# Summing the weights of paired columns by accumulating transfers from GpSimd instead of on VectorE, with two more pairs

## The chip, the core and the metric

The kernel runs on one core of one Trainium2 chip. Its time is the time on the device in microseconds (us), and less is better. In the text PE is TensorE, DVE is VectorE, ACT is ScalarE, POOL is GpSimd and SP is the SyncE queue that issues most transfers. L12 is line 12 of the kernel before.

## What is computed

A decoder trunk of two layers on 528 tokens (512 and 16 learned ones in front) of width 1024. Each layer has a mixer (one projection into two groups of four heads, an output projection) and then a gated MLP, which is where the change lies:

```
def _conv_ffn(h, ffn_up, ffn_conv_w, ffn_conv_b, ffn_down):
    length = h.shape[1]
    u = h @ ffn_up
    up = jnp.pad(u, ((0, 0), (CONV_W - 1, 0), (0, 0)))
    conv = ffn_conv_b + sum(up[:, i:i + length] * ffn_conv_w[i] for i in range(CONV_W))
    a, g = jnp.split(conv, 2, axis=-1)
    return (jax.nn.gelu(a, approximate=True) * g) @ ffn_down
...
    for i in range(DEPTH):
        m = _mixer(_rmsnorm(h, pre_mix_norm[i]), ...)
        h = h + _rmsnorm(m, post_mix_norm[i])
        f = _conv_ffn(_rmsnorm(h, pre_ffn_norm[i]), ffn_up[i], ffn_conv_w[i], ffn_conv_b[i], ffn_down[i])
        h = h + _rmsnorm(f, post_ffn_norm[i])
```

`ffn_up` is 1024 x 5632 per layer in float32: 22 columns of 128 for `a` and 22 for `g`. Column i of `a` and column i of `g` belong together, because their results are multiplied.

## The kernel before

**Products.** Activations lie with the model's width on the 128 partitions and the tokens along the free dimension. Every float32 product is made of float16 parts: a weight is split into a high and a low half, and so is the activation, and three matmuls (high by high, high by low, low by high) stand for one. ACT makes the high half of a weight (an ACTIVATE with a scale), DVE the low one (a SCALAR_TENSOR_TENSOR).

**Blocks.** `plan` lists every weight block of the program in the order of its use. A plain block is 1024 rows by 128 columns (`Block`): one load of 512 KB on SP (L104) into a float32 buffer ("stage cell", `st`), one conversion on ACT (L123) and one on DVE (L131) into a float16 buffer (`unit`). There are ten `unit` buffers (`UNITS`), taken in turn in the order of the blocks, so a block is converted when PE has finished with the block ten places earlier. There are eight stage cells for layer 0 and five for layer 1 (`STAGES`), also taken in turn; a load goes out as soon as its cell has been converted, so loads run further ahead than conversions. `block` asks for up to ten blocks beyond the one in use (`AHEAD`). Loads on SP keep the program's order. ACT and DVE take most of their work in an order that the compiler's list scheduler fixes ahead of the run; each engine then goes through its own list strictly in turn, and an instruction that waits holds up all behind it on that engine.

**A plain column of the up projection** is two blocks, `a` and `g` (`one` in `ffn_up`), each multiplied by the tokens in two parts: 0 to 232 (from 14 on in layer 1) and 232 to 528. ACT copies each product out of PSUM (L1353). After both blocks, `finish` runs the convolution (ACT L1337, DVE L1342), the Gelu (ACT L1393), the product of both (DVE L1404) and, in layer 0, its split into float16 parts (ACT L463, DVE L464).

**A pair** does the same two columns by Strassen's method in Winograd's form, with seven products in place of eight. The weights of column i are seen as a 2 x 2 block matrix: rows 0 to 511 and 512 to 1023 by column `a` and column `g`, so w11, w12 (upper half of `a` and `g`), w21, w22 (lower half). The tokens are halved too (264 each). Seven products of four row blocks of 128, with three matmuls each (12 matmuls over 264 tokens), need w11, w22, w21 and these sums: w11 + w12, w12 + w22, w11 + w12 + w22, and the sum of all four. `paired` runs the products, ACT copies three of them out of PSUM (L1304) and one result (L1326), DVE makes three sums of products (L1308). The sums of activations are made once per layer by `input_sums`. Columns 0 to 4 are always plain; `PAIRED` says which of the others are pairs.

**The weights of a pair** come as four pieces (`PairPiece`), each a unit of its own, taken in the order of steps 0 to 3: w11 with w22; w11 + w12 with w12 + w22; w11 + w12 + w22 with w21; the sum of all four. The products use them in the order 0, 1, 2, 0, 1, 2, 3. At step 0 four loads of 256 KB (L209) fill two stage cells, [w11, w22] and [w12, w21]. At steps 1 to 3 DVE adds in place with four TENSOR_TENSORs (L215), and ACT (L230) and DVE (L231) convert: one conversion of 1024 elements per partition at step 0, two of 512 at steps 1 and 2, one at step 3. Both cells are held until step 3 has been converted.

**Order around it.** PE's order is the compiler's as well: a pair's last product (12 matmuls) often runs inside the next column. PSUM has three banks for these products; the first product's bank is used again by the third. A dependency written by hand (`"sums first"` in `paired`) keeps a piece ten places ahead from being converted before the third product has been copied. POOL takes part in the norms (L459, L492, L514) before and after the up projections, and in L1468, two transfers of 256 KB at the end of the second one.

Of the kernel before, what the change touches and what calls it, by code (L numbers as in the profile page):

```python
# [9 lines left out]
F32 = mybir.dt.float32  # L10
U8 = mybir.dt.uint8
AF = mybir.ActivationFunctionType  # L12
ALU = mybir.AluOpType

P = 128
# [30 lines left out]
SLOTS = 41  # L46
AHEAD = 10
# [21 lines left out]
PAIRED = {0: (9, 11, 13, 14, 15, 17, 19, 20, 21), 1: (8, 10)}  # L69
HK2 = KD // 2  # L70
# [117 lines left out]
class PairPiece:  # L188
# [10 lines left out]

    def fetch(self):  # L200
        if self.unit is not None:
            return
        kern, nc = self.kern, self.kern.nc
        if self.step == 0:
            self.st = []
            for half in (((0, 0), (1, 1)), ((0, 1), (1, 0))):
                st = cell(kern.stage, [P, 2, HK2, P], F32, *kern.stage_of(self.layer))
                for i, (a, b) in enumerate(half):
                    load = nc.sync.dma_start(st[:, i], self.src[512 * a : 512 * (a + 1), self.cols[b] : self.cols[b] + P].rearrange("(k p) c -> p k c", p=P))  # L209
                    kern.tc.keep_in_program_order(load)  # L210
                self.st += [st[:, 0], st[:, 1]]
                if len(self.st) == 2:
                    self.both = st
        w = self.first.st
        add = lambda to, x: nc.vector.tensor_tensor(out=w[to], in0=w[to], in1=w[x], op=ALU.add)  # L215
        if self.step == 0:
            parts = [(slice(0, 2), self.both)]
        elif self.step == 1:
            add(0, 2)
            add(2, 1)  # L220
            parts = [(0, w[0]), (1, w[2])]
        elif self.step == 2:
            add(0, 1)
            parts = [(0, w[0]), (1, w[3])]
        else:
            add(0, 3)
            parts = [(0, w[0])]
        u = self.unit = cell(kern.wpool, [P, 2, 2, HK2, P], F16, "unit", "unit", UNITS)
        for i, st in parts:
            self.hi = nc.scalar.activation(u[:, 0, i], st, AF.Copy, scale=SW)  # L230
            nc.vector.scalar_tensor_tensor(out=u[:, 1, i], in0=st, scalar=SW, in1=u[:, 0, i], op0=ALU.mult, op1=ALU.subtract)  # L231


class Kern:
# [495 lines left out]
    def plan(self):  # L730
        a = self.a
# [7 lines left out]
        for l in range(DEPTH):  # L739
# [4 lines left out]
            for i in range(KF):  # L744
                if i in PAIRED[l]:
                    first = None
                    for q in range(4):
                        self.key[l, "pair", i, q] = len(self.blocks)
                        self.blocks.append(PairPiece(self, l, a["ffn_up"][l], (P * i, DFF + P * i), q, first))
                        first = first or self.blocks[-1]  # L750
                    continue
# [889 lines left out]
```

## Time and profile before

| | |
|---|---|
| median of 3 runs | 1195.14 us (1195.05 to 1195.2) |
| profiled execution | 1195.35 us, span 1193.5 us |
| granted TensorE clock | 1.000 |
| PE, DVE, ACT, POOL busy | 99%, 74%, 57%, 15% |
| HBM read, written | 120.24 MB, 2.10 MB |
| loads of `ffn_up`, plain | 66 of 512 KB, median 4.8 us to landing |
| loads of `ffn_up`, pairs | 44 of 256 KB, median 3.4 us to landing |

The span is the time from the first to the last instruction of the profiled execution; a little lies around it. The page gives busy shares, busy time in 40 slices of the span (about 30 us each), DMA queues, the chain of work that ended last, the costliest groups of instructions, and DMA issues with their time to landing. Other views answer for a stretch of time alone. Matmuls are pipelined: one shows 0.27 us although the next starts after about 0.11 us, so a pair is timed by the distance between its matmuls' starts. Pairs are the groups of line L1296. They lie from 362 to 495 us in layer 0 and from 940 to 973 us in layer 1.

### The profile page before, as it was taken

To read this page: it belongs to the slowest core of one execution; us is meant where nothing else is said; L and a number is where in the kernel's file an instruction comes from. 1 tells how busy PE (TensorE), PEld (TensorE's weight loads), DVE (VectorE), ACT (ScalarE), POOL (GpSimd) and SP (SyncE) were. 2 spreads that over 40 slices of the span, in tenths; PEclk is the share of its full clock that TensorE was granted. 3 is DMA by queue.
4 is the path that set the end of the run, shared out by engine and by line. 5 is a ranking of instruction groups with operands and counts; after the bars stand their busy time and mean duration, and the time that the engine had idled before them with its cause. 6 is when DMAs were issued, how large, how long until landed. Compare 5 with 4: busy or idle time off the path is not lost.

```text
span 1193.5 us, 26242 instructions
## 1 busy us (share of the span) xinstructions
PE 1183.8 (99%) x10910; PEld 998.4 (84%) x10910; DVE 879.8 (74%) x1539; ACT 682.5 (57%) x1351; POOL 184.1 (15%) x213
## 2 busy tenths in 40 slices
PE   8999999999999999999999999999999999999998
PEld 8888889989888888988888888899888888886445
DVE  6687855368998999833565968553799998797687
ACT  6685444564876676633346854445657676664452
POOL 2132311263000000000331414012620000000000
PEclk9999999999999999999999999999999999999999
DMA  8933131122613242642235132211422453206371
GB/s 224 276 108 96 54 90 54 37 65 78 177 36 89 77 119 74 184 112 77 80 99 142 55 89 72 72 54 37 124 71 72 125 164 110 99 1 225 117 250 71
DMA packets 207066, 124.02 MB, mean 104 GB/s; under 512 B 6928, under 2 KB 194500, under 8 KB 206948
## 3 DMA queue, kind: packets, MB, share of 16 engines
q1 hardware_dynamic: 206356, 121.37, 34.8%
q8 instruction: 85, 1.39, 0.5%
q0 software_dynamic: 160, 0.52, 0.1%
q10 hardware_dynamic: 432, 0.46, 0.1%
q14 instruction: 33, 0.27, 0.1%
HBM read 120.24 MB, written 2.10 MB: 103 GB/s over the span
## 4 chain that ended last, share of the span: by engine, by line
PE 87%; DVE 3%; issue 1%; ACT 1%; POOL 1%; POOLq 0%; DVEq 0%; ACTq 0%
PE pu L535 10%; PE pu L534 10%; PE pu L536 10%; PE pl L1480 8%; PE pp L1296 7%; PE pj L534 6%; PE pj L535 6%; PE pj L536 6%; PE pd L534 3%; PE pd L536 3%; PE pd L535 3%; PE po L534 2%; PE po L536 2%; PE po L535 2%; PE o L851 1%
## 5 line engine op out<-in xcount | busy, mean ns | idle before, releaser
L536 PE MATMUL pu<-every,unit 128*128 128x296 f16 (+2 forms) x1056 | 289.1, 274 | 0.0
L535 PE MATMUL pu<-every,unit 128*128 128x296 f16 (+2 forms) x1056 | 289.0, 274 | 0.0
L534 PE MATMUL pu<-every,unit 128*128 128x296 f16 (+2 forms) x1056 | 288.7, 274 | 0.0
L534 PEld LDWEIGHTS <-unit 128*128 128x128 f16 x2508 | 246.1, 98 | 35.4
L536 PEld LDWEIGHTS <-unit 128*128 128x128 f16 x2508 | 245.3, 98 | 36.2
L535 PEld LDWEIGHTS <-unit 128*128 128x128 f16 x2508 | 245.3, 98 | 35.5
L534 PE MATMUL pj<-every,unit 128*128 128x296 f16 (+2 forms) x888 | 244.3, 275 | 0.0
L535 PE MATMUL pj<-every,unit 128*128 128x296 f16 (+2 forms) x888 | 244.3, 275 | 0.0
L536 PE MATMUL pj<-every,unit 128*128 128x296 f16 (+2 forms) x888 | 244.2, 275 | 0.0
L131 DVE SCALAR_TENSOR_TENSOR unit<-st,unit 128x1024 f16<-128x1024 f32 (+2 forms) x161 | 196.7, 1229 | 43.5 <-ACT unit L123 43.3
L123 ACT ACTIVATE unit<-st 128x1024 f16<-128x1024 f32 x159 | 164.9, 1041 | 44.9 <-PE pd L536 20.4
L459 POOL TENSOR_TENSOR every<-every 128x5 f32<-128x5 f32 (+6 forms) x31 | 37.3, 1205 | 556.3 <-DVE every L458 463.2
L1296 PEld LDWEIGHTS <-unit 128*128 128x128 f16 x924 | 90.4, 98 | 14.0 <-issue 0.4
L492 DVE TENSOR_TENSOR acc<-acc,sq 128x296 f32<-128x296 f32 (+2 forms) x60 | 32.3, 541 | 75.0 <-ACT sq L490 69.5
L536 PE MATMUL pd<-av,unit 128*128 128x232 f16 (+1 forms) x308 | 84.7, 276 | 0.0
L535 PE MATMUL pd<-av,unit 128*128 128x232 f16 (+1 forms) x308 | 84.6, 276 | 0.0
L534 PE MATMUL pd<-av,unit 128*128 128x296 f16 (+1 forms) x308 | 84.4, 276 | 0.0
L1353 ACT ACTIVATE u<-pu 128x296 f32<-128x296 f32 (+2 forms) x132 | 49.8, 378 | 49.2 <-PE pu L536 48.0
L1480 PE MATMUL pl<-unit,fk 128*128 128x512 f16 x330 | 71.4, 379 | 0.0
L1342 DVE SCALAR_TENSOR_TENSOR cg<-u,every,cg 128x527 f32<-128x527 f32 (+1 forms) x88 | 66.3, 754 | 4.7 <-ACT cg L1337 4.3
L536 PE MATMUL po<-merged,unit 128*128 128x296 f16 (+2 forms) x256 | 69.7, 274 | 0.0
L535 PE MATMUL po<-merged,unit 128*128 128x296 f16 (+2 forms) x256 | 69.7, 274 | 0.0
(279 smaller groups left out, 1938.9 us busy)
## 6 DMA issues: line engine op xcount, KB each, us to landing
st<-in_ffn_up SPq DMA_DIRECT2D x66, 512.0 KB, 4.8
st<-in_w_in SPq DMA_DIRECT2D x56, 512.0 KB, 4.1
st<-in_ffn_down SPq DMA_DIRECT2D x46, 512.0 KB, 4.9
st<-in_ffn_up SPq DMA_DIRECT2D x44, 256.0 KB, 3.4
st<-in_w_out SPq DMA_DIRECT2D x16, 512.0 KB, 4.1
st<-in_ffn_down SPq DMA_DIRECT2D x8, 384.0 KB, 6.7
out<-yo SPq DMA_DIRECT2D x7, 256.0 KB, 2.0
w<-in_ffn_down SPq DMA_DIRECT2D x3, 512.0 KB, 5.1
```

What stands on the lines that cost most here:

```text
L123: self.hi = self.kern.nc.scalar.activation(self.unit[:, 0], self.st, AF.Copy, scale=SW)
L131: self.last = self.kern.nc.vector.scalar_tensor_tensor(out=out, in0=x, scalar=SW, in1=high, op0=ALU.mult, op1=ALU.subtract)
L459: nc.gpsimd.tensor_tensor(out=r[:w, :n], in0=t[:w, :n], in1=self.mhalf[:w, :n], op=ALU.pow)
L492: self.summed = eng.tensor_tensor(out=acc[:, :n], in0=acc[:, :n], in1=sq[:, :n], op=ALU.add)
L534: nc.tensor.matmul(ps[:, :n], w[:, 0, kk, :], x[:, 0, n0:n1], start=first, stop=False)
L535: nc.tensor.matmul(ps[:, :n], w[:, 0, kk, :], x[:, 1, n0:n1], start=False, stop=False)
L536: nc.tensor.matmul(ps[:, :n], w[:, 1, kk, :], x[:, 0, n0:n1], start=False, stop=last)
L851: nc.tensor.matmul(o[:, i, :], intra(i + 1), vn(i + 1), start=i == 0, stop=i == 0, skip_group_check=i > 0)
L1296: mm = lambda p, q, **kw: nc.tensor.matmul(ps, u[:, p, k, :], x[k][:, q], skip_group_check=more, **kw)
L1342: nc.vector.scalar_tensor_tensor(out=to, in0=u[:, max(lo, d) - d : L - d], scalar=self.cvec[:, ci(i) : ci(i) + 1], in1=to, op0=ALU.mult, o ...
L1353: nc.scalar.activation(u[:, n0:n1], ps[:, : n1 - n0], AF.Copy, scale=IXW)
L1480: mm = lambda x, w, **kw: nc.tensor.matmul(ps[:, cols], x, w[:, cols], skip_group_check=more, **kw)
```

## The change

Three things.

1. The sums are no longer made by DVE. `load` issues six loads of 256 KB on SP: w11 and w22, w12 and w21 as before, and w11 twice more into a third buffer [wa, wd]. That buffer is a cell of its own in layer 0 (`wx`, four of them, in the `keep` pool) and a third stage cell in layer 1. `sums` issues transfers from POOL that add to what lies in their destination (`accum_op`). At step 0: w12, once more from HBM, to wa; w22 to w12; w21 to wd; then the new w12 to wd. At step 1: the new w12 to w11. They keep the program's order on POOL. The pieces that are converted have the same values as before: wa is w11 + w12, the new w12 is w12 + w22, the new w11 is w11 + w12 + w22, wd is the sum of all four.
2. In `plan` each pair's first piece changes places with the block ahead of it (the `g` block of a plain column, or the last piece of the pair ahead), so it is loaded and converted one place earlier.
3. `PAIRED` in layer 0 goes from nine columns to ten, two pairs and then a plain column, with four pairs at the end; in layer 1 from two columns to three.

```diff
+WX = 4
...
-PAIRED = {0: (9, 11, 13, 14, 15, 17, 19, 20, 21), 1: (8, 10)}
+PAIRED = {0: (9, 10, 12, 13, 15, 16, 18, 19, 20, 21), 1: (8, 10, 12)}
...
+    def load(self):
+        kern, nc = self.kern, self.kern.nc
+        more = (kern.keep, "wx", "wx", WX) if self.layer == 0 else (kern.stage, *kern.stage_of(self.layer))
+        cells = [cell(pool, [P, 2, HK2, P], F32, *tag) for pool, *tag in [(kern.stage, *kern.stage_of(self.layer))] * 2 + [more]]
+        quarter = lambda a, b: self.src[512 * a : 512 * (a + 1), self.cols[b] : self.cols[b] + P].rearrange("(k p) c -> p k c", p=P)
+        order = ((0, 0, 0, 0), (0, 1, 1, 1), (1, 0, 0, 1), (2, 0, 0, 0), (1, 1, 1, 0), (2, 1, 0, 0))
+        for c, i, a, b in order:
+            load = nc.sync.dma_start(cells[c][:, i], quarter(a, b))
+            kern.tc.keep_in_program_order(load)
+        (w11, w22), (w12, w21), (wa, wd) = ((c[:, 0], c[:, 1]) for c in cells)
+        self.parts = [(slice(0, 2), cells[0])], [(0, wa), (1, w12)], [(0, w11), (1, w21)], [(0, wd)]
+        self.adds = [(wa, quarter(0, 1)), (w12, w22), (wd, w21), (wd, w12)], [(w11, w12)], [], []
+
+    def sums(self, step):
+        for to, x in self.adds[step]:
+            add = self.kern.nc.gpsimd.dma_start(out=to, in_=x, accum_op=ALU.add)
+            self.kern.tc.keep_in_program_order(add)
+
     def fetch(self):
...
-        w = self.first.st
-        add = lambda to, x: nc.vector.tensor_tensor(out=w[to], in0=w[to], in1=w[x], op=ALU.add)
-        if self.step == 0:
-            parts = [(slice(0, 2), self.both)]
-        elif self.step == 1:
-            add(0, 2)
-            add(2, 1)
-            parts = [(0, w[0]), (1, w[2])]
-        elif self.step == 2:
-            add(0, 1)
-            parts = [(0, w[0]), (1, w[3])]
-        else:
-            add(0, 3)
-            parts = [(0, w[0])]
+            self.load()
+        self.first.sums(self.step)
+        parts = self.first.parts[self.step]
...
                         first = first or self.blocks[-1]
+                    n = self.key[l, "pair", i, 0]
+                    self.blocks[n - 1 : n + 1] = self.blocks[n - 1 : n + 1][::-1]
+                    self.key = {k: {n - 1: n, n: n - 1}.get(v, v) for k, v in self.key.items()}
                     continue
```

More of the change, by code (lines that the diff above doesn't have):

```diff
@@ L204, in fetch @@
         if self.step == 0:
[L205 to L213, printed above, removed]
-        w = self.first.st
-        add = lambda to, x: nc.vector.tensor_tensor(out=w[to], in0=w[to], in1=w[x], op=ALU.add)
-        if self.step == 0:
-            parts = [(slice(0, 2), self.both)]
-        elif self.step == 1:
-            add(0, 2)
-            add(2, 1)
-            parts = [(0, w[0]), (1, w[2])]
-        elif self.step == 2:
-            add(0, 1)
-            parts = [(0, w[0]), (1, w[3])]
-        else:
-            add(0, 3)
-            parts = [(0, w[0])]
+            self.load()
+        self.first.sums(self.step)
+        parts = self.first.parts[self.step]
         u = self.unit = cell(kern.wpool, [P, 2, 2, HK2, P], F16, "unit", "unit", UNITS)
```

## The prediction

> **What bounds the kernel now.** First the page: its span, the engines' shares and the busy slices.
>
> ```profile
> span 1193.5 us, 26242 instructions
> ...
> PE 1183.8 (99%) x10910; PEld 998.4 (84%) x10910; DVE 879.8 (74%) x1539; ACT 682.5 (57%) x1351; POOL 184.1 (15%) x213
> ...
> PE   8999999999999999999999999999999999999998
> ...
> DVE  6687855368998999833565968553799998797687
> ```
>
> PE is 99% busy in a span of 1193.5 us; the profiled execution took 1195.35 us, 1.85 us around that span, and the median of the runs is 1195.14 us. DVE shows 9s in slices 9 to 14, which is where the first up projection lies. So PE sets the end, and DVE is nearest to taking its place. The table of stretches says how near, in the first (388 to 500) and second up projection (920 to 980).
>
> ```profile
> core 0: us, PE busy (x) PEld busy (x) DVE busy (x) ACT busy (x) POOL busy (x), PEclk, DMA share, GB/s
> 388.00:418.00 30.00, 30.00 (x269) 26.09 (x268) 27.27 (x42) 20.55 (x37) 0.00 (x0) 1.00 0.28 79
> 448.00:478.00 30.00, 30.00 (x269) 26.10 (x267) 28.98 (x48) 20.44 (x39) 0.00 (x0) 1.00 0.28 79
> 478.00:500.00 22.00, 21.80 (x205) 19.86 (x204) 20.74 (x29) 14.95 (x23) 0.00 (x0) 1.00 0.80 225
> 920.00:980.00 60.00, 60.00 (x544) 52.17 (x542) 58.29 (x88) 44.73 (x77) 0.00 (x0) 1.00 0.49 141
> ```
>
> The granted clock is 1.00 everywhere. In 388 to 418 and 448 to 478 PE is busy for all 30.00 us although DVE stands at 27 to 29 of 30. POOL has 0.00: it does nothing there. Only 478 to 500 misses 0.20 us. The waits of PE put a name to it (line, waited for, us in total, times, longest), and the chain and ACT's timeline show the place.
>
> ```profile
> PE o L851 <- DVE sn L938: 0.6, 2, 0.3
> PE pp L1296 <- ACT part L1304: 0.2, 1, 0.2
> ```
>
> ```profile
> 479.20 2.73 ACT L123 ACTIVATE unit<-st 128x768 f16<-128x768 f32 x3
> 481.82 0.63 ACT L1393 ACTIVATE ca<-ca 128x528 f32<-128x528 f32 x1
> 482.36 0.38 ACT L1304 ACTIVATE part<-pp 128x264 f32<-128x264 f32 x1
> ```
>
> ```profile
> 362.43 8.10 PE pp L1296 x72
> ...
> 382.68 8.10 PE pp L1296 x72
> ...
> 402.93 27.00 PE pp L1296 x240
> ...
> 442.08 8.10 PE pp L1296 x72
> ...
> 482.78 6.91 PE pp L1296 x60
> ```
>
> A copy of a product out of PSUM (L1304) started at 482.36, after three weight conversions (L123) and a Gelu, and PE went on only then. That is all that PE loses in pairs: 0.2 us. So inside the pairs matmul count is time, and nothing else is worth more than 0.2 us.
>
> **The matmuls of the added pairs.** In the chain above 240 matmuls of pairs take 27.00 us, 112.5 ns each. A pair has 7 products of 12, so 84 matmuls and 9.45 us. Pair 9 begins at 362.43 and pair 11 at 382.68; between them lie one pair and one plain column, so a plain column is 20.25 - 9.45 = 10.80 us. Pairs 13, 14, 15 and plain 16 agree: 442.08 - 402.93 = 39.15 = 3 x 9.45 + 10.80. In the second layer, whose first half is narrower:
>
> ```profile
> 939.58 8.10 PE pp L1296 x72
> ...
> 959.55 8.10 PE pp L1296 x72
> ```
>
> 959.55 - 939.58 = 19.97, less 9.45 leaves 10.52. The first layer goes from 9 pairs to 10, the second from 2 to 3: 1.35 + 1.07 = **2.42 us** less on PE, all of it on the path as PE has no idle time there. Where the pairs stand (by twos, and 18 to 21 in a row) does not change PE's count.
>
> **The sums leave DVE.** What conversions, sums and copies cost:
>
> ```profile
> L215 DVE TENSOR_TENSOR st<-st x44: 678/684/693, 322.0 to 942.4; 128x512 f32<-128x512 f32 x44
> ```
>
> ```profile
> L231 DVE SCALAR_TENSOR_TENSOR unit<-st,unit 128x512 f16<-128x512 f32 x40 | 26.6, 685 | 3.3 <-ACT unit L230 3.1
> L230 ACT ACTIVATE unit<-st 128x512 f16<-128x512 f32 x40 | 23.9, 623 | 13.7 <-DVE st L215 12.8 <-PE pu L536 0.6
> L131 DVE SCALAR_TENSOR_TENSOR unit<-st,unit 128x1024 f16<-128x1024 f32 x13 | 15.8, 1222 | 1.6 <-ACT unit L123 1.6
> L230 ACT ACTIVATE unit<-st 128x1024 f16<-128x1024 f32 x8 | 8.4, 1046 | 0.3 <-PE pp L1296 0.3
> L1308 DVE SCALAR_TENSOR_TENSOR u<-pp,part 128x264 f32<-128x264 f32 x27 | 11.1, 424 | 1.9 <-ACT unit L123 1.1 <-ACT unit L230 0.8
> ```
>
> ```profile
> ACT unit L230 <- DVE st L215: 12.8, 13, 3.1
> ```
>
> Removed: 44 x 0.684 = 30.1 us of DVE. Each added pair gives DVE one conversion of 1.22 and five of 0.685 in place of two of 1.222, and three sums of products at 0.424 (L1308): 4.65 - 2.44 + 1.27 = 3.5 us, 7.0 for both. All this lies beside PE, which already kept its pace with DVE fuller; the worth is the 0.2 us stall at most. ACT waited 12.8 us for L215 in 13 places, up to 3.1 us at once, and all that PE lost meanwhile is the 0.2. With the sums done by transfers those waits of ACT go, and the copy at 482.36 comes earlier; I count **0.2 us** for it. What is late next on ACT is then the transfers themselves, below; if they keep it waiting as long, the 0.2 stays.
>
> **What the transfers cost.** No accumulating transfer is in this trace. The nearest rows are SP's loads of the same 256 KB, and POOL's two transfers of 256 KB late in the kernel (L1468).
>
> ```profile
> q1 hardware_dynamic: 206356, 121.37, 34.8%
> ...
> st<-in_ffn_up SPq DMA_DIRECT2D x44, 256.0 KB, 3.4
> ...
> every<-in_post_ffn_norm POOLq DMA_DIRECT2D x2, 256.0 KB, 7.2
> ```
>
> ```profile
> L1468 POOL DMA_DIRECT2D every<-in_post_ffn_norm x2: 554/648/742, 1084.6 to 1085.3; - x2
> ...
> DMA to landing us min/median/max: 6.9/7.2/7.5
> ```
>
> Landing lies between 3.4 us (SP's load) and twice 7.2 us = 14.4 (POOL's, if reading the destination too doubles it); I take 7.2, the row of the same queue and size. At 3.4 nothing more is gained, since PE has no idle time left to give. The issue takes 0.65 us of POOL, up to four times that, 2.6, for the one whose source in HBM has rows of 512 bytes, not 2 KB.
>
> *The w11 sum* is the tight one: it may be issued only when the pair's first piece has been converted, and the third piece's conversion needs it landed. The change moves the first piece one block ahead, so three conversions' turns lie between. In pair, pair, plain ten blocks take 29.70 us, 2.97 each; three turns less the first piece's own conversion (1.05 on ACT, then 1.22 on DVE) leave 6.6 us. Four pairs in a row have 9.45 / 4 = 2.36 a block, so 4.8. Issue and landing are 7.85 us: ACT would wait 1.2 us at a pair of a two and 3.0 at one of the four. Behind that wait stand ACT's copies of products. Both are under the 3.1 us that cost PE nothing, so I cost this at 0; the cover is the ten units converted ahead, 23.6 us of pairs.
>
> *POOL's queue* holds nothing but these sums in both up projections, so only sums wait behind a waiting sum. A pair's round is: w11 issue 0.65, wa 2.6, two more 1.3, landing 7.2, the second wd issue 0.65, so 12.4 us. Two pairs and a plain column give 29.70 for two rounds. In the four, (12.4 - 9.45) x 3 = 8.9 us is lost against 23.6 of units ahead: hidden.
>
> *SP* issues six loads a pair in place of four; a row of four takes 2.05 us, so 0.51 each. Now they stand far ahead:
>
> ```profile
> 301.18 2.05 SPq L209 DMA_DIRECT2D st<-in_ffn_up  x4
> ```
> ```profile
> 433.01 2.92 SPq L209 DMA_DIRECT2D st<-in_ffn_up  x4
> ```
> ```profile
> 890.15 2.05 SPq L209 DMA_DIRECT2D st<-in_ffn_up  x4
> ```
>
> Pair 9's loads go out at 301.18, 61 us before its first matmul; the last pair's at 433 to 436, 462.33 + 2 x 9.45 = 481.2 less that is over 45 us ahead (462.33 = 442.08 + 9.45 + 10.80); in the second layer 939.58 - 890.15 = 49 us. The longest path, six loads (3.1 + 3.4), then two sums one after the other (2 x 7.85), is 22.2 us. The first layer's third buffer is new room (wx, four of them); if an older tile still holds it, the first load waits, and the 61 us cover that too. In the second layer three of five cells hold a pair, and the next pair's loads wait for the last piece: with that piece's conversion (0.62 + 0.685) 23.5 us a round against 19.97, 7.1 us lost in two rounds, hidden by 49.
>
> *The DMA engines.* q1's 121.37 MB took 34.8% of the span, 415 us: 3.42 us a MB. A pair's four loads of 0.262 MB took 3.6 us; six take 5.4, five sums 4.5 if priced like loads and 9.0 if double: 9.9 to 14.4 us in 9.45. Two pairs and a plain column: 23.4 to 32.4 of 29.70 us. From 362 on, ten pairs and three plain columns need at the double price 154.8 us, PE takes 126.9; 27.9 us are lost against a lead of 45. The Trainium skill ("Collectives: The Full Stack", the bandwidth ceiling) says that an add in the DMA engines reads two sources and so moves half the bytes per time, which is the double price; no run here shows it yet.
>
> Sum: 2.42 + 0.20 = 2.62 us off the span, 1190.9, so 1192.7 for an execution like the profiled one, and 1195.14 - 2.62 = **1192.5 us** beside the median.
>
> **The rivals.**
>
> *A copy comes late now and then (same).* The next product but one needs the copied bank, 1.35 us later, of which the copy itself takes 0.38; a copy right behind a 3.0 us wait makes PE wait 3.0 - 0.97 = 2.0 us. Once in the run of four: 1192.5 + 2.0 = 1194.5 us. For it: the copy at 482.36, late behind ACT's other work. Against it: 13 waits of ACT cost PE nothing.
>
> *The w11 sum lands late (slower).* Place: ACT's conversion of each third piece. At a landing of T us a pair of the four loses T + 0.65 - 4.8 - 3.1 = T - 7.25, each of the nine others T - 9.05. The gain is gone at T = 7.9, slower by over 0.2% at 8.5; T = 10 gives 4 x 2.75 + 9 x 0.95 = 19.6, so 1212 us; T = 9 gives 1199.5. For it: 6.9 to 7.5 us for a plain transfer of POOL's. Against it: those are two transfers at one place, and 3.1 us is only the longest harmless wait seen, not a limit.
>
> *The DMA engines fill (slower).* At the double price the lead of 45 us falls to 17; two sums that also land in 14.4 need 6.5 + 30.1 + 1.3 for the last piece, 37.9, and are wanted 8.1 us (six products) after the pair begins. 37.9 - 8.1 - 17 = 12.8 us: 1205 us. Against it: only the end of the run of four could show it, as the plain columns give DMA time back.
>
> *DVE holds up POOL (same).* In the trace POOL's two issues fell where DVE was idle, from 1084.57 to 1086.42, so none is shown beside DVE:
>
> ```profile
> 1084.59 1.30 POOL L1468 DMA_DIRECT2D every<-in_post_ffn_norm  x2 [210.05 <-DVE ca L1342]
> ```
>
> ```profile
> 1083.03 1.54 DVE L1342 SCALAR_TENSOR_TENSOR ca<-u,every,ca 128x512 f32<-128x512 f32 x2 [1.43 <-ACT ca L1337]
> 1086.42 1.54 DVE L1342 SCALAR_TENSOR_TENSOR cg<-u,every,cg 128x512 f32<-128x512 f32 x2 [1.85 <-ACT cg L1337]
> ```
>
> If each of five issues waited for one DVE instruction of 1.22 us, POOL's round would be 18.5, (18.5 - 9.45) x 3 = 27.2 us lost in the four against 23.6 ahead: 3.6 us, 1196.1. Against it: 512 elements take 0.685 us and 1024 take 1.22, about 1.05 ns an element, and no form is twice as fast as another. The Trainium skill ("SBUF — State Buffer", Who interferes with whom) has this rule: a DVE instruction in a two-port fast mode shuts GpSimd out, which then cannot write descriptors; by these rates DVE is in no such mode here.
>
> **How the numbers follow.** The forecast has 0.47, the late copy 0.28, DVE against POOL 0.03, the late sum 0.16, full DMA engines 0.06. A measurement of this kernel can tell about 0.2%, 2.4 us, from no change. The forecast is 2.62 us below, just past that: faster 0.47; same 0.28 + 0.03 = 0.31; slower 0.16 + 0.06 = 0.22. The low end, 1191.9, lets a new order of the work take away also the 0.6 us that PE waits for L938. The high end, 1200.0, takes in the late copy, POOL held up, and the late sum up to a landing of 9 us; left out are slower landings (0.10) and full DMA engines (0.06). The faster case alone has 1191.9 to 1192.7.
>
> **What would show it.** Right: L1296 has 84 x 13 = 1092 matmuls; pairs stand 9.45 us apart, or 20.25 and 19.97 across a plain column; PE is full in every stretch of both up projections; L215 is gone, DVE falls by some 23 us; ACT's waits for transfers stay under 3.1 us each; accumulating transfers land in about 7 us. Wrong: PE waiting for L1304, with ACT's L230 waiting for POOL's transfers (late sum); landings that grow along 18 to 21 with the DMA share near 1 (full engines); POOL issues of over 1.2 us beside a busy DVE.

## The result, and the profile after

The changed kernel takes 1209.94 us (1208.66 to 1211.14) beside 1195.17 us for the kernel before: 1.0123 times as long, 95% interval 1.011 to 1.0135. It is slower, and outside the range given. The profiled execution took 1208.66 us, with a span of 1206.9 us against 1193.5. Lines below are those of the kernel after: L216 issues the accumulating transfers, L229 and L230 convert a pair's pieces on ACT and DVE, L1298 are the pairs' matmuls, L1306 ACT's copies of products.

The page of the kernel after:

```profile
span 1206.9 us, 26450 instructions
...
PE 1186.1 (98%) x10886; PEld 998.3 (83%) x10886; DVE 860.2 (71%) x1509; ACT 685.2 (57%) x1359; POOL 246.7 (20%) x278
...
PE   8999999999999888999999999999999999999998
...
q1 hardware_dynamic: 220148, 128.19, 36.0%
q0 software_dynamic: 14512, 17.57, 9.1%
```

The three 8s in a row, slices 14 to 16, are where the time went. PE has 24 matmuls fewer, and DVE 19.6 us less to do, and yet PE is no longer full there. The stretches of the first up projection:

```profile
core 0: us, PE busy (x) PEld busy (x) DVE busy (x) ACT busy (x) POOL busy (x), PEclk, DMA share, GB/s
388.00:418.00 30.00, 26.53 (x220) 22.11 (x218) 23.54 (x36) 20.50 (x37) 5.33 (x6) 0.94 0.86 183
418.00:448.00 30.00, 26.47 (x221) 22.13 (x219) 20.45 (x30) 17.89 (x33) 9.76 (x10) 0.94 0.90 188
448.00:478.00 30.00, 26.62 (x224) 22.33 (x223) 23.98 (x38) 18.50 (x34) 11.46 (x12) 0.94 1.05 216
```

Each loses about 3.5 us of PE, and the granted clock falls to 0.94. No engine is near its limit: DVE has 20 to 24 us in 30, less than before. (The DMA share, 0.86 to 1.05, is the time of all packets added up, divided by 16 engines and the stretch, and can pass 1; what it costs is tried below.) So PE waits for something that itself waits. PE's own waits and its timeline at the first of these places:

```profile
PE pp L1298 <- ACT part L1306: 11.2, 6, 3.5
```
```profile
394.95 1.51 PE L1298 MATMUL pp<-every,unit 128*128 128x264 f16 x12
399.93 5.88 PE L1298 MATMUL pp<-xs,unit 128*128 128x264 f16 x36 [3.47 <-ACT part L1306]
405.64 0.61 PE L1298 MATMUL pp<-every,unit 128*128 128x264 f16 x4
```

PE waits 3.47 us for a copy out of PSUM. Then 36 matmuls take 405.64 - 399.93 = 5.71 us instead of 36 x 0.1125 = 4.05: 15 of them stand 220 ns apart, not 112.5, because the clock was halved: 3.4 us at half speed in each stretch of 30 make the mean of 0.94. By the distances between the matmuls' starts there are three such places: 3.63, 3.70 and 3.38 us of waiting (at 396.2, 431.2 and 466.0 us), with 15, 13 and 11 slow matmuls behind them. The waits are 10.71 us. The slow matmuls cost 39 x (0.220 - 0.1125) = 4.2 us, with those at their edges 4.4. With 1.45 us of small waits (0.33 in layer 0, 0.47 and 0.65 in layer 1) that makes 16.6 us. Less the 0.37 of the kernel before and the 2.42 of the matmuls that are gone, that is 13.8; the span grew by 13.4.

Why is the copy late? ACT's timeline ahead of it, and a window of its busy time:

```profile
375.38 0.63 ACT L229 ACTIVATE unit<-st 128x512 f16<-128x512 f32 x1 [1.44 <-DMA st<-st]
...
380.63 1.15 ACT L229 ACTIVATE unit<-st 128x512 f16<-128x512 f32 x2 [0.45 <-DMA st<-st]
390.32 0.63 ACT L229 ACTIVATE unit<-st 128x512 f16<-128x512 f32 x1 [6.77 <-DMA st<-st]
399.51 0.37 ACT L1306 ACTIVATE part<-pp 128x264 f32<-128x264 f32 x1
```
```profile
390.30:399.60 9.30, 6.16 (x53) 5.02 (x52) 8.47 (x13) 8.27 (x16) 0.86 (x1) 1.00 0.91 203
```

At 390.32 ACT converts the third piece of pair 13, after waiting 6.77 us for the accumulating transfer that makes it, the w11 sum. PE is ten units behind, in pair 12. The copy that it wants, of a product of pair 12, is the last of the 16 instructions in that window, which keep ACT busy for 8.27 of 9.30 us: the work that the wait has held up. At the other two places the waits are 6.71 and 5.31 us. And why was the sum late? POOL's timeline, and DVE's conversions of the first pieces of pairs 12 and 13:

```profile
371.44 0.86 POOL L216 DMA_DIRECT2D st<-st  x1 [22.58 <-DVE unit L230]
372.04 1.58 POOL L216 DMA_DIRECT2D wx<-in_ffn_up  x1
372.80 1.74 POOL L216 DMA_DIRECT2D st<-st  x1
373.34 2.08 POOL L216 DMA_DIRECT2D wx<-st  x1
383.59 0.88 POOL L216 DMA_DIRECT2D wx<-st  x1 [8.17 <-DMA st<-in_ffn_up]
384.16 1.20 POOL L216 DMA_DIRECT2D st<-st  x1
```
```profile
369.92 1.22 DVE L230 SCALAR_TENSOR_TENSOR unit<-st,unit 128x1024 f16<-128x1024 f32 x1
...
377.33 1.23 DVE L230 SCALAR_TENSOR_TENSOR unit<-st,unit 128x1024 f16<-128x1024 f32 x1 [0.60 <-ACT unit L229]
```

The first row is the w11 sum of pair 12. POOL stood 22.58 us for it, until pair 12's first piece had been converted (369.92 + 1.22 = 371.14). Only then come pair 13's four other sums; the second one into wd, which needs the new w12 and the first sum into wd, stands 8.17 us for landings (the name in brackets is only the releaser that the trace infers; the last of them, of the first sum into wd, came 9.7 us after its issue, at 383.05). The last row is pair 13's w11 sum. Its own first piece had been converted at 377.33 + 1.23 = 378.56; it goes out at 384.16 and is there at 390.32.

ACT wanted pair 12's sum at 375.38 - 1.44 = 373.94 and pair 13's at 390.32 - 6.77 = 383.55, 9.61 us apart. POOL sent them 384.16 - 371.44 = 12.72 us apart, and from issue to use they took 3.94 and 6.16 us. 1.44 + (12.72 - 9.61) + (6.16 - 3.94) = 6.77 us: the whole wait.

### The profile page after: what moved, and what is told of

The parts are those of the page before. It is cut to its first block, busy times and chain, and to the rows that moved or that the text cites. A ratio compares the mean times of both kernels' runs of the same rounds, so it can differ in the third digit from the quotient of the medians.

```text
span 1206.9 us, 26450 instructions
## 1 busy us (share of the span) xinstructions
PE 1186.1 (98%) x10886; PEld 998.3 (83%) x10886; DVE 860.2 (71%) x1509; ACT 685.2 (57%) x1359; POOL 246.7 (20%) x278
## 3 DMA queue, kind: packets, MB, share of 16 engines
q1 hardware_dynamic: 220148, 128.19, 36.0%
q0 software_dynamic: 14512, 17.57, 9.1%
## 5 line engine op out<-in xcount | busy, mean ns | idle before, releaser
L535 PE MATMUL pu<-every,unit 128*128 128x296 f16 (+2 forms) x992 | 271.6, 274 | 0.0
L534 PE MATMUL pu<-every,unit 128*128 128x296 f16 (+2 forms) x992 | 271.5, 274 | 0.0
L533 PE MATMUL pu<-every,unit 128*128 128x296 f16 (+2 forms) x992 | 271.2, 274 | 0.0
L132 DVE SCALAR_TENSOR_TENSOR unit<-st,unit 128x1024 f16<-128x1024 f32 (+1 forms) x157 | 191.6, 1226 | 53.6 <-ACT unit L124 53.4
L124 ACT ACTIVATE unit<-st 128x1024 f16<-128x1024 f32 x155 | 160.8, 1041 | 58.2 <-PE pd L535 17.3
L1298 PEld LDWEIGHTS <-unit 128*128 128x128 f16 x1092 | 108.9, 100 | 30.4 <-issue 12.2
L1298 PE MATMUL pp<-xs,unit 128*128 128x264 f16 x624 | 79.5, 286 | 11.2 <-ACT part L1306 11.2
```

The costliest lines, as they stand in the source:

```text
L124: self.hi = self.kern.nc.scalar.activation(self.unit[:, 0], self.st, AF.Copy, scale=SW)
L132: self.last = self.kern.nc.vector.scalar_tensor_tensor(out=out, in0=x, scalar=SW, in1=high, op0=ALU.mult, op1=ALU.subtract)
L533: nc.tensor.matmul(ps[:, :n], w[:, 0, kk, :], x[:, 0, n0:n1], start=first, stop=False)
L534: nc.tensor.matmul(ps[:, :n], w[:, 0, kk, :], x[:, 1, n0:n1], start=False, stop=False)
L535: nc.tensor.matmul(ps[:, :n], w[:, 1, kk, :], x[:, 0, n0:n1], start=False, stop=last)
L1298: mm = lambda p, q, **kw: nc.tensor.matmul(ps, u[:, p, k, :], x[k][:, q], skip_group_check=more, **kw)
```

## The experiments

*Theory A* of the expectations: the w11 sum goes out late, since POOL takes its sums strictly in turn and stands at waits for conversions and for landings. *Theory B*: the transfers as such are the cost (bytes, full DMA engines, slow landings). A kernel "on DVE" makes a sum as before, with a TENSOR_TENSOR. Each ratio is to the kernel before on the same chip; the runs come from four chips, so rows are best compared by their ratios.

| run | us | ratio to before, 95% interval |
|---|---|---|
| w11_on_dve | 1195.49 | 1.0001 (0.9992 to 1.0011) |
| next_pair_first | 1210.18 | 1.0126 (1.0111 to 1.0142) |
| old_pairs | 1197.75 | 1.0021 (1.0011 to 1.003) |
| all_on_dve | 1193.75 | 0.9987 (0.9978 to 0.9996) |
| own_buffer | 1197.02 | 1.0014 (1.0005 to 1.0023) |
| wd_on_dve | 1235.11 | 1.0332 (1.0317 to 1.0348) |
| wa_only | 1192.8 | 0.9979 (0.997 to 0.9988) |
| no_swap | 1211.41 | 1.014 (1.0126 to 1.0154) |
| w11_before_wd | 1212.57 | 1.0141 (1.0126 to 1.0157) |
| wa_w12 | 1191.9 | 0.9969 (0.9958 to 0.9981) |
| wa_eleven | 1198.5 | 1.0024 (1.0014 to 1.0035) |
| none_adjacent | 1198.04 | 1.0023 (1.0013 to 1.0032) |

**w11_on_dve**: the w11 sum alone goes back to DVE.

```diff
-        self.adds = [(wa, quarter(0, 1)), (w12, w22), (wd, w21), (wd, w12)], [(w11, w12)], [], []
+        self.adds = [(wa, quarter(0, 1)), (w12, w22), (wd, w21), (wd, w12)], [], [], []
+        self.last_sum = w11, w12
...
+        if self.step == 2:
+            w11, w12 = self.first.last_sum
+            nc.vector.tensor_tensor(out=w11, in0=w11, in1=w12, op=ALU.add)
```

> The sum into w11 goes back to DVE (one addition of 0.68 us per pair, at the third piece); the other four sums stay transfers. Theory A, POOL's queue: the kernel is slow because the w11 sum waits on POOL for a conversion and holds up the next pair's sums behind it, so those are issued some 23 us late and ACT then waits 5 to 7 us for a landing. Without it POOL's sums wait for loads alone: the three stalls of PE of 3.4 to 3.7 us go, and the time is 1192 to 1195 us. Theory B, the transfers are simply too slow or the DMA engines too full: four of five sums remain, the third piece still needs the sum into w12, so ACT still waits for landings and the time stays above 1203 us.

14.5 us come back with one sum of five; the time is just above theory A's range of 1192 to 1195 and far below theory B's 1203. The stretches, in the same columns as above:

```profile
388.00:418.00 30.00, 30.00 (x268) 26.06 (x267) 26.60 (x42) 21.50 (x39) 7.91 (x8) 1.00 1.00 209
418.00:448.00 30.00, 30.00 (x269) 26.06 (x267) 26.63 (x41) 21.90 (x38) 8.16 (x9) 1.00 1.10 244
```

PE is full although the DMA share is higher than in the changed kernel. What is left are two waits of 1.44 and 1.17 us in layer 1 and one of 0.60 in layer 0.

**next_pair_first**: the next pair's loads and its first four sums are issued ahead of this pair's w11 sum, so that they do not stand behind its wait.

```diff
+            early = self.first.then if self.step == 1 else None
+            for piece in (early, self):
+                if piece and piece.step == 0 and not piece.loaded:
+                    piece.load()
+                    piece.sums(0)
...
+                    if i - 1 in PAIRED[l]:
+                        self.blocks[self.key[l, "pair", i - 1, 0]].then = first
```

> The same transfers, loads and pairs as in the changed kernel; only POOL's order differs: where two pairs follow one another, the next pair's loads and its first four sums are issued ahead of this pair's w11 sum. Theory A: the second pair's sums no longer stand behind a wait of 10 to 23 us, its w11 sum finds w12 landed and goes out as soon as its first piece is converted; stalls gone or under 1 us each, 1193 to 1198 us. Theory B: as many bytes through the same engines, so no change: 1206 to 1213 us.

A miss for theory A as it was put; the time lies in theory B's range. POOL's timeline (line 217 here) tells why:

```profile
332.05 0.86 POOL L217 DMA_DIRECT2D wx<-st  x1 [9.86 <-DMA wx<-st]
332.58 1.20 POOL L217 DMA_DIRECT2D st<-st  x1
```

Pair 9's w11 sum now stands behind pair 10's sum into wd, which waits 9.86 us for a landing. That sum is there at 337.6, after a wait of ACT of 11.0 us. PE stalls 5.2 us at 366 us and 4.6 us at 464; that the first of these follows from the 11.0 us is argued, not shown. The hold only moved: in this order too a pair's sums stand behind another's wait.

**old_pairs**: the transfers, but the columns paired in the kernel before.

```diff
-PAIRED = {0: (9, 10, 12, 13, 15, 16, 18, 19, 20, 21), 1: (8, 10, 12)}
+PAIRED = {0: (9, 11, 13, 14, 15, 17, 19, 20, 21), 1: (8, 10)}
```

> The sums by transfers and the swapped first piece stay, but the pairs are those of the kernel before (9, 11, 13, 14, 15, 17, 19, 20, 21 and 8, 10). Theory A: single pairs (9, 11, 17) cost nothing; in each run of three the second pair's sums stand behind the first one's w11 sum: two to three stalls of about 5 us with the slower clock after them, so 1195.2 plus 10 to 16: 1205 to 1211 us. Theory B: fewer sums, spread wider, so the DMA engines have more room: well below the changed kernel, 1197 to 1202 us.

The time is the one that theory B gave; the run by itself speaks for B. ACT's waits for the w11 sums are shorter here, and what old_pairs says of the account is taken up in the next section. ACT's waits, and PE's, from 350 to 510 us:

```profile
ACT unit L229 <- DMA st<-st: 9.0, 5, 3.9
PE pp L1298 <- ACT part L1306: 1.1, 3, 0.5
```

**all_on_dve**: all sums on DVE, with the new pairs and the change of places kept.

```diff
-            self.load()
-        self.first.sums(self.step)
-        parts = self.first.parts[self.step]
+            self.st = []
...
+        elif self.step == 1:
+            add(0, 2)
+            add(2, 1)
+            parts = [(0, w[0]), (1, w[2])]
...
```

> The new pairs and the swapped first piece alone: all sums on DVE, as before. If pairs are worth what PE's count says, 2.4 us, and DVE keeps pace by twos: 1192.7 us. If DVE is over its limit (about 12 us of work in a pair of 9.45): PE loses in the run of four, by some 1 to 5 us: 1194 to 1198 us. In neither case the stalls of 3.5 us at the second pair of a two.

So the pairs and the change of places alone are worth 1.6 us: less than PE's 2.42, as there are new waits of 1.05 and 0.53 us near 470 to 492 us. Over the whole kernel ACT waited 15.3 us in 17 places for DVE's sums before; with 13 pairs in place of 11 it is 17.1 in 20:

```profile
ACT unit L230 <- DVE st L215: 17.1, 20, 2.8
```

**own_buffer**: in layer 0 all five sums by transfer, but the last goes into a third copy of w11 in a buffer of its own, so that no sum waits for a conversion. That is a load more a pair, and one stage cell and one `wx` less to make room.

```diff
...
-        self.parts = [(slice(0, 2), cells[0])], [(0, wa), (1, w12)], [(0, w11), (1, w21)], [(0, wd)]
+        wt = cells[2][:, 2] if own else w11
+        self.parts = [(slice(0, 2), cells[0])], [(0, wa), (1, w12)], [(0, wt), (1, w21)], [(0, wd)]
+        if own:
+            self.adds = [*self.adds[0], (wt, w12)], [], [], []
```

> In layer 0 the w11 sum gets a buffer of its own: w11 is loaded once more there (a seventh load) and w12's sum is added to it with the other sums at step 0, so all five sums remain transfers but none waits for a conversion. To make room there are three wx buffers in place of four and seven stage cells in place of eight. Layer 1 is as in the changed kernel. Theory A (the w11 sum, released by a conversion and queued on POOL among sums that wait for landings, comes too late for ACT): the three long stalls go although more bytes are moved: 1193 to 1198 us. Theory B (transfers too slow, DMA engines too full): more bytes, so no better or worse: 1208 us or more.

13 us come back with more bytes. A stretch, and ACT's wait:

```profile
418.00:448.00 30.00, 30.00 (x269) 26.05 (x267) 25.41 (x39) 21.82 (x38) 10.27 (x12) 1.00 1.17 256
```
```profile
ACT unit L233 <- DMA wx<-st: 5.2, 3, 3.1
```

A DMA share of 1.17 with PE full for all 30.00 us: as the cause of the three long stalls theory B falls. One wait of PE of 2.16 us at 472 us stays, in the run of four, and ACT waits up to 3.1 us for landings, so late landings still cost something.

**wd_on_dve**: the opposite of w11_on_dve. The second sum into wd goes to DVE, so that the w11 sum has nothing in front of it that waits for a sum of its own pair.

```diff
-        self.adds = [(wa, quarter(0, 1)), (w12, w22), (wd, w21), (wd, w12)], [(w11, w12)], [], []
+        self.adds = [(wa, quarter(0, 1)), (w12, w22), (wd, w21)], [(w11, w12)], [], []
+        self.last_sum = wd, w12
...
+        if self.step == 3:
+            wd, w12 = self.first.last_sum
+            nc.vector.tensor_tensor(out=wd, in0=wd, in1=w12, op=ALU.add)
```

> The second sum into wd, which waited on POOL for two landings, goes to DVE at the fourth piece; the w11 sum stays a transfer. As many transfers as with the w11 sum on DVE. Theory A: the w11 sum must still wait for w12's landing and for the conversion, but goes out some 3.6 us earlier at the second pair of a two; ACT's waits fall from 6.8 to about 3 us and PE's stalls to under 1 us each: 1196 to 1201 us. Theory B, where only the number of transfers counts: the same as with the w11 sum on DVE, 1195.5 us, with no waits of ACT left.

A miss for both theories, and the slowest of all. The waits of DVE and POOL (lines 229 and 217 here):

```profile
POOL st L217 <- DVE unit L234: 154.7, 10, 35.9
DVE wx L229 <- DMA wx<-st: 31.5, 10, 4.8
```

Now DVE waits for POOL's transfers, and POOL's transfers for DVE's conversions. DVE's sum is held by the first sum into wd, which stood on POOL behind a wait for DVE. PE has waits of up to 6.62 us.

**wa_only**: in layer 0 one sum by transfer, w11 + w12, into a buffer of its own from HBM; DVE makes the other three, and all four in layer 1. The edit is against all_on_dve.

```diff
+            self.wa = self.st[0]
+            if self.layer == 0:
+                self.wa = cell(kern.keep, [P, HK2, P], F32, "wx", "wx", WX)
+                quarter = lambda b: self.src[:512, self.cols[b] : self.cols[b] + P].rearrange("(k p) c -> p k c", p=P)
+                kern.tc.keep_in_program_order(nc.sync.dma_start(self.wa, quarter(0)))
+                kern.tc.keep_in_program_order(nc.gpsimd.dma_start(out=self.wa, in_=quarter(1), accum_op=ALU.add))
...
```

> New pairs and swapped first piece; in layer 0 only the sum w11 + w12 is a transfer (a fifth load of w11 into a buffer of its own, w12 added from HBM), which depends on its own load alone; DVE makes the other three sums, and all in layer 1. Theory A: no chain of landings and no wait for a conversion, so no wait of ACT; DVE has 0.68 us less per pair, and the stalls of 1.0 and 0.5 us that all sums on DVE left in the run of four shrink: 1192.3 to 1193.5 us. Rival: any accumulating transfer in this stretch costs PE something (POOL against DVE, fuller DMA engines): above the 1193.75 us of all sums on DVE.

As expected, and faster than the kernel before. It is also below all_on_dve (1193.75), but the two intervals overlap.

**no_swap**: the changed kernel without the change of places in `plan`.

```diff
-                    n = self.key[l, "pair", i, 0]
-                    self.blocks[n - 1 : n + 1] = self.blocks[n - 1 : n + 1][::-1]
-                    self.key = {k: {n - 1: n, n: n - 1}.get(v, v) for k, v in self.key.items()}
```

> The changed kernel without the change of places: a pair's first piece is loaded and converted right ahead of its second. If the conversion of the first piece is what releases the w11 sum too late, one turn (2.4 to 3 us) is lost at each of 13 pairs: ACT's waits grow by that and the time goes to 1215 to 1235 us. If the queue on POOL alone sets the w11 sum's time, the swap does not matter: 1207 to 1213 us.

It takes no less, so the change of places is not what made the kernel slow, and the second range comes out. The waits are not the same, though. From 350 to 510 us ACT waits 19.9 us in 9 places (25.7 in 10 with the change of places), and PE's waits in layer 0 near 396, 430 and 465 to 482 us add up to 9.2 us in place of 11.0; in layer 1 one of 4.41 us has come, at 952 us.

**w11_before_wd**: two sums of a pair change places on POOL, nothing else.

```diff
-        self.adds = [(wa, quarter(0, 1)), (w12, w22), (wd, w21), (wd, w12)], [(w11, w12)], [], []
+        self.adds = [(wa, quarter(0, 1)), (w12, w22), (wd, w21)], [(w11, w12), (wd, w12)], [], []
```

> The changed kernel with two transfers of each pair in the other order on POOL: the w11 sum now stands ahead of wd's second sum, which waits for wd's first to land. Same transfers, bytes, pairs, and PE order. Theory A (the w11 sum is issued late because it stands in POOL's line behind a sum that waits about 10 us for landings): the w11 sum goes out as soon as its own first piece is converted, so at the second pair of a two ACT's wait falls from 6.7 us to under 3 us, no stall of PE in layer 0 is over 2 us and 1193 to 1198 us come out. Rival: it is the waits for conversions in front, not the wait for landing, that make the w11 sum late (POOL stands up to 22.6 us before the previous pair's w11 sum); then the sums of the next pair go out as late as now, stalls of 3 us and more stay and it takes 1204 to 1212 us. By the number of bytes or packets: 1209, as the changed kernel.

Theory A in this form falls. What the rival says comes out: PE's three stalls are 3.3 to 4.8 us, and the time is 0.6 us above the rival's range. POOL's and ACT's timelines at the same place as above:

```profile
371.72 0.86 POOL L216 DMA_DIRECT2D st<-st  x1 [31.85 <-DVE u L1310]
372.26 1.20 POOL L216 DMA_DIRECT2D wx<-st  x1
372.80 2.00 POOL L216 DMA_DIRECT2D wx<-in_ffn_up  x1
373.55 2.15 POOL L216 DMA_DIRECT2D st<-st  x1
...
382.11 0.88 POOL L216 DMA_DIRECT2D st<-st  x1 [5.53 <-DVE cg L1344]
384.24 0.87 POOL L216 DMA_DIRECT2D wx<-st  x1 [1.25 <-DMA wx<-st]
```
```profile
388.27 0.63 ACT L229 ACTIVATE unit<-st 128x512 f16<-128x512 f32 x1 [3.99 <-DMA st<-st]
...
391.02 0.63 ACT L229 ACTIVATE unit<-wx 128x512 f16<-128x512 f32 x1 [1.84 <-DMA wx<-st]
```

Pair 13's w11 sum goes out at 382.11, only 2.05 us earlier than before, and the sum into wd is late in its place: ACT waits 3.99 and 1.84 us. The first piece had been converted at 378.77; what the w11 sum still needs is the new w12, issued at 373.55, which by the view of DMA issues landed 8.0 us later, at 381.6 (the row names a DVE instruction, but that is only the inferred releaser). So it is not the place behind wd's sum. It is that nothing of pair 13 may start before 371.72, when pair 12's w11 sum is released, and that from there an issue, a landing, an issue and a landing follow.

**none_adjacent**: the test of this revised theory. All transfers stay as they are, but no pair of layer 0 stands directly behind another.

```diff
-PAIRED = {0: (9, 10, 12, 13, 15, 16, 18, 19, 20, 21), 1: (8, 10, 12)}
+PAIRED = {0: (9, 11, 13, 15, 17, 19, 21), 1: (8, 10, 12)}
```

> The changed kernel with all its transfers, but in layer 0 the pairs are 9, 11, 13, 15, 17, 19, 21: no pair stands directly behind another, each has 20.25 us. Three pairs fewer cost PE 3 x 1.35 = 4.05 us. Revised theory (the w11 sum ties POOL to the conversion of each pair's first piece, and the next pair's chain of issues and two landings, some 12.5 us, starts only then; a pair 9.45 us behind it is too late, one 20.25 us behind is not): ACT's longest wait for a transfer is under 3.1 us in layer 0, no stall of PE over 1 us there, 1191.9 + 4.05 and 1.1 us of layer 1: 1195.5 to 1198 us. Rival (any wait of POOL for a conversion makes the w11 sum late, whatever the distance; or transfers disturb ACT's and DVE's work as such): waits of 5 us and more and stalls of 3 us at some pairs, 1203 us or more.

```profile
388.00:418.00 30.00, 30.00 (x274) 26.55 (x272) 22.89 (x33) 20.32 (x35) 8.83 (x9) 1.00 0.85 178
418.00:448.00 30.00, 30.00 (x264) 25.64 (x263) 24.89 (x37) 20.67 (x38) 5.72 (x6) 1.00 0.96 208
448.00:478.00 30.00, 30.00 (x275) 26.61 (x273) 22.12 (x32) 19.39 (x33) 0.86 (x1) 1.00 0.44 114
```
```profile
POOL st L216 <- DVE unit L230: 50.3, 5, 17.8
```

PE is full, and between 350 and 510 us ACT has no wait for a transfer at all, though POOL still waits up to 17.8 us for conversions. The time is at the upper end of the range that the revised theory gave. That it stands 2.6 us above the kernel before has another cause: two pairs fewer in layer 0 and one more in layer 1 give PE 2 x 1.35 - 1.07 = 1.63 us more to do, and it waits 1.7 us in layer 1. With fewer pairs there are fewer transfers too, so by itself this run doesn't part the distance from their number; own_buffer, with more of them, does. Together they say that the distance between pairs decides (more exactly in the next section).

**wa_w12 and wa_eleven**: as wa_only, with w12 + w22 by transfer as well, the second sum that waits for no conversion; and as wa_only, with column 17 of layer 0 an eleventh pair. First the edit of wa_w12, then that of wa_eleven, both against wa_only.

```diff
+                kern.tc.keep_in_program_order(nc.gpsimd.dma_start(out=self.st[2], in_=self.st[1], accum_op=ALU.add))
...
-            if self.layer:
-                add(0, 2)
-            add(2, 1)
+            if self.layer:
+                add(0, 2)
+                add(2, 1)
```
```diff
-PAIRED = {0: (9, 10, 12, 13, 15, 16, 18, 19, 20, 21), 1: (8, 10, 12)}
+PAIRED = {0: (9, 10, 12, 13, 15, 16, 17, 18, 19, 20, 21), 1: (8, 10, 12)}
```

> As wa_only (1192.8 us: in layer 0 one sum of each pair, w11 + w12, by a transfer into a buffer of its own), but a second sum that waits for no conversion, w22 to w12, goes by a transfer too; DVE makes the other two of layer 0, all four in layer 1. Theory A (transfers cost PE nothing as long as POOL never waits for a conversion or for another sum): 1192.3 to 1193.5 us, POOL waits for loads alone. Rival (each further sum on the transfers makes ACT or DVE wait for landings): stalls of PE of 1 us and more at the second pieces, 1194 us or more.

> As wa_only, with column 17 of layer 0 a pair as well: eleven pairs, the last seven columns but none plain from 15 on. If PE's count of matmuls is the whole cost, 1.35 us less than wa_only: 1191.4 us. If DVE (three sums, six conversions and three sums of products a pair in 9.45 us, 3 x 0.68 + 1.22 + 5 x 0.685 + 3 x 0.42 = 7.9 us before the convolution's and Gelu's share) has no room in seven pairs in a row, PE waits 2 to 6 us: 1193.5 to 1198 us. I expect the second.

wa_w12 is the fastest, 3.6 us under the kernel before (the interval reaches from 2.3 to 5.0 us) and a little under the range expected. Its PE waits for copies 0.2 us in all, as before the change. With eleven pairs PE loses 7.6 us, more than the 2 to 6 expected. In the second stretch below DVE is full; in the first it is not, and PE waits there for both DVE's sums of products and ACT's copies. First wa_w12, then two stretches of wa_eleven:

```profile
PE pp L1308 <- ACT part L1316: 0.2, 1, 0.2
```
```profile
420.00:450.00 30.00, 27.43 (x240) 23.27 (x238) 25.92 (x43) 19.73 (x38) 2.76 (x3) 1.00 0.59 131
450.00:480.00 30.00, 28.32 (x251) 24.34 (x250) 30.00 (x51) 21.45 (x41) 0.00 (x0) 1.00 0.31 91
```

## Why the prediction was wrong, point by point

**The step that failed** is *The w11 sum*: "ACT would wait 1.2 us at a pair of a two", and so "I cost this at 0". It counted from the conversion of the pair's own first piece, as if POOL were free then. For the second pair of a two the wait was 6.77, 6.71 and 5.31 us, over the 3.1 us taken as harmless, and it cost PE 3.4 to 3.7 us each time. The half clock behind these stalls cost 4.4 us more in all, for which the prediction had no term.

For the first pair of a two the number came out (1.44 us at pair 12, 1.63 and 1.56 at 15 and 18), but by luck. At pair 12 issue and landing were put at 7.85 us and took 375.38 - 371.14 = 4.24. The cover was put at 6.6 us, as three mean turns less the first piece's conversion, and was 373.94 - 371.14 = 2.80. The mean misleads here: by the order of the blocks, pieces of pair 9 stand ten places ahead of pair 12's first and third piece, and only two products, 2.7 us, lie between PE's last use of one and of the other.

**POOL's queue** had the number that was needed. A round was put at 12.4 us and measured 384.16 - 371.44 = 12.72, again with errors that cancel: the four issues up to the first sum into wd started within 1.90 us, where 4.55 were counted, and the second sum into wd followed 10.25 us later, where 7.2 were. But "two pairs and a plain column give 29.70 for two rounds" averages over a two as if POOL could work ahead through the plain column. It can't: the w11 sum at the end of each pair's sums ties it to that pair's first conversion, so the second pair's chain begins only there, and 12.4 us are set against the 9.45 us to the next pair (7.42 us between the conversions of the two first pieces). With the prediction's own numbers the wait would have been 1.2 + 12.4 - 9.45 = 4.2 us, already over 3.1; the slower landing of the second sum makes up most of the rest. none_adjacent and own_buffer show both ends of this: with 20.25 us between pairs, or with no wait for a conversion, the long waits are gone.

**The matmuls** were right: 1092 of them in L1298, 24 fewer in all. wa_w12 gives what they are worth when nothing new waits. Its span is 3.2 us shorter; 1.4 and 1.1 us of that are gained in the two up projections, where 1.35 and 1.07 were forecast, and the rest elsewhere, 0.35 of it after the last matmul, where nothing was changed.

**DVE** lost 19.6 us, not 23. That it had no part in PE's pace was right for the pairs of before; with ten pairs and all sums on DVE new waits of 1.6 us appear (all_on_dve), so taking two sums off it is worth about 1.9 us (1193.75 against 1191.9, on different chips, with intervals that just overlap). The prediction's reading that DVE shows 9s in slices 9 to 14 was off: they are slices 11, 12 and 14 to 16, still in the first up projection, and nothing hangs on it.

**Landing** was taken at 7.2 us. DMA issues of the whole kernel, then those under way at 371.5 us (pair 12's w11 sum) and at 373.5 (pair 13's first three sums):

```profile
st<-st POOLq DMA_DIRECT2D x32, 256.0 KB, 6.1
wx<-st POOLq DMA_DIRECT2D x20, 256.0 KB, 7.2
wx<-in_ffn_up POOLq DMA_DIRECT2D x10, 256.0 KB, 7.4
```
```profile
st<-st POOLq DMA_DIRECT2D x1, 256.0 KB, 3.9
```
```profile
wx<-in_ffn_up POOLq DMA_DIRECT2D x1, 256.0 KB, 7.2
st<-st POOLq DMA_DIRECT2D x1, 256.0 KB, 7.8
wx<-st POOLq DMA_DIRECT2D x1, 256.0 KB, 9.7
```

The medians fit. So the rival that named this place had the right place and the wrong cause: the w11 sums landed in 3.9 and 6.1 us at pairs 12 and 13, while its arithmetic needed over 8.5; they were sent late. The 9.7 us of the first sum into wd are part of why, as POOL stood for that landing.

**The DMA engines** did not fill to a point that explains the long stalls (own_buffer). The double price was about right: q0's 17.57 MB took 9.1% of 16 engines' span, 110 us or 6.25 us a MB, against 434 us for 128.19 MB, 3.39 a MB, on q1. This agrees with the Trainium skill ("Collectives: The Full Stack", the bandwidth ceiling), whose rule gives a factor of 2 where the trace has 1.8.

**DVE against POOL**: the four issues from 371.44 on start 0.54 to 0.76 us apart beside a busy DVE. The rival fell.

**Distance, more exactly.** In old_pairs 14, 15, 20 and 21 stand directly behind another pair, and yet in layer 0 ACT's longest wait is 3.9 us and PE's 0.5. In the changed kernel's run of four only pair 19 waits long. By the revised theory each should have. DVE's timelines explain most of it. POOL is released by the conversion of a first piece, and that follows what PE is at ten units earlier, not the pair's own place. In the changed kernel the first pieces of 12 and 13, 15 and 16, 18 and 19 were converted 7.42, 7.39 and 7.47 us apart, well under POOL's round of 12.72, and these are the three long waits. Those of 20 and 21 came 14.61 and 13.65 us after the one ahead, and neither waited long.

In old_pairs the first pieces of 14 and 20 came 18.3 and 18.0 us after the one ahead. Those of 15 and 21 came after 7.8 and 7.5 us; but there ACT reached the third piece only some 9.5 us after the first had been converted (5.0 us in pair 13 of the changed kernel), when the late sum had landed or was about to. The wait of 3.9 us is pair 19's, whose sum went out at once and took 7.25 us to land.

**What stays open.** So two things count: how far apart the first pieces are converted, and how soon after it the third is wanted. This is read from the traces; no run changed the one and kept the other. Why PE lost only 0.5 us behind the wait of 3.9, and nothing behind some of 3.1, was not looked into.

## What to carry to other kernels

A transfer that waits for a conversion makes an in-order queue wait at the pace of its consumer, and the queue can then no longer work ahead: set its round against the shortest distance between two releases, not against their mean (here 12.7 against 7.4 us). Move to such a queue the steps that wait for loads alone (in wa_w12 two sums of four, with which the kernel is 0.3% faster than before), and give a step that overwrites a buffer still being read a buffer of its own or leave it on an engine. When a wait grows past what its cover holds, look for whose copy or result stands behind it; here it was an instruction 9 us further down ACT's list.

## What the runs showed of the hardware that was not expected

**A stall of PE can cost half as much again.** In the up projections of all these kernels, after each of the twelve stalls of 3.3 us or more, 11 to 26 matmuls ran at half the clock (those of a pair 220 ns apart); after the twenty-one of 1.0 to 2.2 us none did; of five between 2.36 and 2.86 us, those of 2.36, 2.43 and 2.61 us were followed by 14 to 17 slow ones and those of 2.46 and 2.86 by none. So the length alone doesn't decide in that range. The Trainium skill ("TensorE: Matmul & The Clock Gate", Part 1: The HAM clock gate) states half rate after at least one idle window of about 3.4 us; the long stalls agree, while a stall of 2.36 us that halved the clock is shorter than that window.

**A POOL issue is cheap, its landing is not.** The row of one issue of an accumulating transfer of 256 KB shows 0.85 us or more, yet the next starts 0.54 to 0.76 us after it. But a sum that needs others waits for their landing: pair 13's second sum into wd went out 383.59 - 373.34 = 10.25 us after the first. And landing grows with what is sent just ahead: of the four issued within 1.9 us from 371.44 on, the first landed in 3.9 us and the others in 7.2, 7.8 and 9.7; the fours from 406.57 and 441.30 on went alike (4.0 and 4.1 us for the first, 9.7 and 9.6 for the last).
